# Three feed-forward first projections with both parts of the features in one 512-column matmul, and the two parts held in one tile

## The chip, the cores and the metric

The kernel runs on one core of one Trainium2 chip. The metric is the device time of one execution in microseconds (us). The engines named below are TensorE (PE for its matmuls, PEld for its weight loads), VectorE (DVE), ScalarE (ACT), GpSimd (POOL) and SyncE (SP, which issues most transfers). Matmuls write to PSUM, the accumulator memory; all other tiles lie in SBUF.

## What is computed

Two blocks run one after the other on 256 tokens with 1024 features. The first block has two layers; the second is one layer that also takes a context of 256 tokens and a condition vector.

```
# first block, for i in range(2):
h = h + concat(pool_mixer, dilated_attention)(rmsnorm(h, norm1[i]) @ w_in[i]) @ w_out[i]
hn = rmsnorm(h, norm2[i])
h = h + jnp.square(jax.nn.relu(hn @ w_up[i])) @ w_down[i]          # 1024 -> 4096 -> 1024
h = h + jax.nn.sigmoid(rmsnorm(h, norm3[i]) @ w_gate[i]) * (p[i] @ w_ple[i])
x = rmsnorm(h, final_norm)
# second block
mod = silu(c) @ w_mod + b_mod                                      # six shifts, scales and gates
h = modulate(x, norm1_g, sh1, sc1); hc = modulate(ctx, ...)
x = x + g1 * branch_merge(h, bidirectional gated delta scan(hc, h), short conv, fourier) @ w_o
a, b = split(modulate(x, norm2_g, sh2, sc2) @ w_ffn_in)            # 1024 -> 2 x 2816
x = x + g2 * ((silu(a) * b) @ w_ffn_out)
out = rmsnorm(x, final_g)
```

## The kernel before

Features lie on the 128 partitions (eight groups, `KD = 8`), the 256 tokens (`T`) along the free dimension. Every large product is made from fp32 values split in two parts, a high part and the rest: weights become `wh` and `wl` (in `weights`: ACT copies, DVE subtracts, in halves of 512 columns), features become `xh` and `xl` (in `split`). `mm3` then makes three matmuls of 256 moving columns for each 128x128 block: `wh` by `xh`, `wh` by `xl`, `wl` by `xh`. One unit of weights is 128x1024, which is eight such steps, 24 matmuls.

The work is a Python program that a scheduler turns into one order of instructions for each engine; each engine then runs its own in that order, and waits on semaphores for what others make. So an instruction that waits holds up all that stand behind it on its engine.

The stages, in order, with the stretch of the profiled execution in us: layer 0's attention with its out projection (0 to 117), its feed-forward `ffn` (to 304) and its gate (to 340); layer 1's the same (attention to 440, `ffn` to 657, gate to 692); the mixer of the second block (692 to 1010); its feed-forward `swiglu` (to 1203); the end. In `ffn`, 16 rounds each take two units of `w_up` into one PSUM bank (`cols_into`), make the squared relu in `square` (`fft`, `ah`, `al`), and take two units of `w_down` of the round before into four accumulators `acc` (`down`). In `swiglu`, 11 rounds each take four units of `w_fin`, and two of `w_fout`.

Three generators run beside these stages, one step at a time when `tick` is called for a unit: `modulation` (48 loads of `w_mod`, 512 KB each, through the tiles `wmst`; DVE multiplies each by a vector and sums), `context` and the delta recurrence (`dn_prep`, `dn_scan`). Inside `dn_prep`, `dn_base` inverts small blocks on POOL, with a way out to DRAM and back (`there`, `back`, `xc`), and then lets `trip` steps pass before `dn_merge` reads `xc` into `Tm` and `U` and multiplies with them:

```
        for _ in range(self.trip):
            yield
        X["X"] = xc
```

The normalization is not applied to the features but to the products: `row_steps` sums the squares of `h` (`ssp`, `ss`), takes the column sums on TensorE, makes the inverse root by DVE in ten small instructions (`rsv`, `rsy`, `rst`), and spreads it over the partitions (`across`); in `ffn` the first `square` needs that row. `residual` adds the accumulators to `h`, after which `norm_split` makes `xh` and `xl` of the next stage. `np2` sends the low part of the first three weights of the mixer (`wl`) to POOL in place of DVE.

## Time and profile before

| | |
|---|---|
| time, median of 3 runs | 1226.24 us (1225.2 to 1228.88) |
| the profiled execution | 1224.34 us, span 1222.2 us, mean granted TensorE clock 0.986 |
| PE busy | 1174.3 us (96%), 9882 matmuls |
| DVE busy | 899.3 us (74%) |
| ACT busy | 635.6 us (52%) |
| POOL busy | 119.9 us (10%) |
| moved by DMA | 221.43 MB |

Busy time of an engine is the time in which the profile shows an instruction on it; matmuls overlap, so the time that one matmul takes from the engine is read from how far apart the starts of neighbours lie, not from its own duration.

### The profile page before, as it was taken

Reading aid. Unit: us, or ns where it says so; the run is one execution under the profiler, and the core shown is the slowest. Engines: PE = TensorE matmul, PEld = TensorE weight load, DVE = VectorE, ACT = ScalarE, POOL = GpSimd, SP = SyncE. Lnnn points to the kernel's source line nnn. Section 1 sums busy time; section 2 is a strip of 40 time slices with the busy share of each in tenths; the row PEclk is TensorE's granted clock in tenths of the full one; section 3 lists DMA queues with packets and bytes.
Section 4 is the critical chain, followed back from the end, with each engine's and each line's share of the span. In section 5 each row is a group of like instructions: output and inputs, shape, how many; then the busy total and the mean of one; then the engine's idle time right before and its main releaser. Section 6 shows DMA issues by size and latency. Waiting matters only on the chain.

```text
span 1222.2 us, 24807 instructions
## 1 busy us (share of the span) xinstructions
PE 1174.3 (96%) x9882; PEld 1111.4 (91%) x9882; DVE 899.3 (74%) x1804; ACT 635.6 (52%) x1250; POOL 119.9 (10%) x207
## 2 busy tenths in 40 slices
PE   8999899999999989999999999997999999999997
PEld 6779899999977889999999979897989998999996
DVE  6998997556998488675657899897655768555555
ACT  5654645545755565644445555544333546544444
POOL 1000000000010000064000130275000000000000
PEclk9999999999999999999999989999999998999998
DMA  6767688555553645556444525677422452655552
GB/s 223 238 199 249 208 297 278 189 194 190 164 174 121 200 139 164 182 165 207 156 147 164 171 91 164 226 270 243 142 89 100 173 195 99 213 185 189 186 180 84
DMA packets 65779, 221.43 MB, mean 181 GB/s; under 512 B 10048, under 2 KB 11456, under 8 KB 65664
## 3 DMA queue, kind: packets, MB, share of 16 engines
q1 hardware_dynamic: 64800, 218.29, 53.4%
q0 software_dynamic: 864, 1.57, 0.6%
q8 instruction: 77, 1.26, 0.4%
q14 instruction: 38, 0.31, 0.1%
HBM read 218.00 MB, written 1.84 MB: 180 GB/s over the span
## 4 chain that ended last, share of the span: by engine, by line
PE 72%; DVE 13%; DMA 6%; POOL 4%; issue 3%; ACT 2%; SPq 0%; DVEq 0%; POOLq 0%; ACTq 0%
PE acc L274 38%; PE bank L274 33%; DVE wl L263 4%; DMA wmst<-w_mod 2%; DVE xl L298 1%; POOL bo L1288 1%; POOL bz L1289 1%; ACT wh L262 1%; DVE wmst L882 1%; PE bank L565 1%; DVE h L704 1%; DVE cy L1044 1%; DMA back<-bzt 1%; DVE qkT L533 1%; DMA pt<-pT 0%
## 5 line engine op out<-in xcount | busy, mean ns | idle before, releaser
L262 ACT ACTIVATE wh<-wst 128x512 fp32r<-128x512 f32 x708 | 411.9, 624 | 427.4 <-PE bank L274 157.3
L263 DVE TENSOR_TENSOR wl<-wst,wh 128x512 fp32r<-128x512 f32 x702 | 470.1, 703 | 208.5 <-ACT wh L262 208.0
L274 PE MATMUL bank<-xl,wh 128*128 128x256 f32 x992 | 280.5, 283 | 2.1 <-DVE xl L298 2.1
L274 PE MATMUL bank<-xh,wl 128*128 128x256 f32 x992 | 279.4, 282 | 2.9 <-DVE wl L263 2.9
L274 PE MATMUL bank<-xh,wh 128*128 128x256 f32 x992 | 281.3, 284 | 0.8 <-ACT wh L262 0.8
L274 PE MATMUL acc<-al,wh 128*128 128x256 f32 x688 | 191.6, 279 | 0.0
L274 PE MATMUL acc<-ah,wl 128*128 128x256 f32 x688 | 191.3, 279 | 0.0
L274 PE MATMUL acc<-ah,wh 128*128 128x256 f32 x688 | 191.2, 279 | 0.0
L274 PEld LDWEIGHTS bank<-xh,wl 128*128 128x128 f32 x992 | 187.0, 189 | 4.3 <-DVE wl L263 4.3
L274 PEld LDWEIGHTS bank<-xl,wh 128*128 128x128 f32 x992 | 187.0, 189 | 2.8 <-DVE xl L298 2.7
L274 PEld LDWEIGHTS bank<-xh,wh 128*128 128x128 f32 x992 | 187.1, 189 | 1.6 <-ACT wh L262 1.2
L274 PE MATMUL acc<-xh,wh 128*128 128x256 f32 x640 | 183.4, 287 | 2.2 <-ACT xh L911 2.2
L274 PE MATMUL acc<-xl,wh 128*128 128x256 f32 x640 | 182.0, 285 | 1.5 <-DVE xl L912 1.5
L274 PE MATMUL acc<-xh,wl 128*128 128x256 f32 x640 | 181.1, 284 | 0.5 <-DVE wl L263 0.4
L274 PEld LDWEIGHTS acc<-al,wh 128*128 128x128 f32 x688 | 129.0, 188 | 0.0
L274 PEld LDWEIGHTS acc<-ah,wl 128*128 128x128 f32 x688 | 128.9, 188 | 0.1
L274 PEld LDWEIGHTS acc<-ah,wh 128*128 128x128 f32 x688 | 128.9, 188 | 0.0
L274 PEld LDWEIGHTS acc<-xh,wh 128*128 128x128 f32 x640 | 121.6, 190 | 4.7 <-ACT xh L911 2.8
L274 PEld LDWEIGHTS acc<-xl,wh 128*128 128x128 f32 x640 | 121.5, 190 | 2.9 <-DVE xl L912 1.7
L274 PEld LDWEIGHTS acc<-xh,wl 128*128 128x128 f32 x640 | 121.9, 191 | 1.5 <-DVE wl L263 0.9
L274 PE MATMUL acc<-wl,xh 128*128 128x512 f32 x176 | 70.6, 401 | 2.5 <-DVE wl L263 2.4
L274 PE MATMUL acc<-wh,xh 128*128 128x512 f32 x176 | 70.8, 406 | 1.1 <-ACT wh L262 1.1
(365 smaller groups left out, 1564.8 us busy)
## 6 DMA issues: line engine op xcount, KB each, us to landing
wst<-w_up SPq DMA_DIRECT2D x64, 512.0 KB, 4.2
wst<-w_down SPq DMA_DIRECT2D x64, 512.0 KB, 4.2
wmst<-w_mod SPq DMA_DIRECT2D x48, 512.0 KB, 4.8
wst<-w_fin SPq DMA_DIRECT2D x44, 512.0 KB, 3.2
wst<-w_in SPq DMA_DIRECT2D x39, 512.0 KB, 3.6
wst<-w_mgate SPq DMA_DIRECT2D x24, 512.0 KB, 3.3
wst<-w_fout SPq DMA_DIRECT2D x22, 512.0 KB, 3.2
wst<-w_qkv SPq DMA_DIRECT2D x20, 512.0 KB, 3.4
```

The source lines that it names most:

```text
L262: nc.scalar.activation(wh[:, c:c + n], st[:, c:c + n], AF.Copy)
L263: i = (nc.gpsimd if self.onpool > 0 else nc.vector).tensor_tensor(wl[:, c:c + n], st[:, c:c + n], wh[:, c:c + n].bitcast(F32), op=OP.subtract)
L274: self.nc.tensor.matmul(out, lhsT, rhs, start=start, stop=stop, skip_group_check=skip)
L298: nc.vector.scalar_tensor_tensor(xl[:, k], src, gain, xh[:, k].bitcast(F32), op0=OP.mult, op1=OP.subtract)
L533: nc.vector.tensor_copy(qk[:, :, t * P:(t + 1) * P], bk.rearrange("p (c q) -> p c q", c=4))
L565: nc.tensor.transpose(bk[:, c * P:(c + 1) * P], s[:, g, c * P:(c + 1) * P], self.ident)
L704: self.nc.vector.tensor_add(h[:, js], h[:, js], acc[j][:, n[0]:n[1]])
L882: nc.vector.scalar_tensor_tensor(pr, st, 1.0, cv[v], op0=OP.mult, op1=OP.mult, accum_out=mod[:, part, v, k:k + 1])
L1044: nc.vector.scalar_tensor_tensor(y4[:, j], pad[:, j, :, tap:tap + CHUNK], w[:, j, tap:tap + 1], y4[:, j], op0=OP.mult, op1=OP.add)
L1288: pool.tensor_tensor(o, lt[:, c:, j:c].to_broadcast([P, n, c]), Z[:, j:c, 0:c].to_broadcast([P, n, c]), op=OP.mult)
L1289: pool.tensor_tensor(Z[:, c:, 0:c], Z[:, c:, 0:c], o, op=OP.subtract)
```

## The change

First, the two parts of the features are one tile (`Pair`, name `xs`), so that one access reaches both. Then the units of `w_up` and of `w_fin` (but for the first four of the latter) go through `wide` in place of `cols_into`: each step is one matmul with `wh` held and 512 moving columns (`xh` and `xl` side by side, into the two halves of a PSUM bank) and one with `wl` held and 256 columns. In all, 832 steps have two matmuls where they had three. A unit so takes a bank of its own, and `merged` adds the two halves: ACT copies one half to SBUF (104 times), DVE adds the other. In `ffn` the relu moves to ACT, and the row of the normalization is applied after `w_down`, in `residual`: the square of the inverse root is a plain reciprocal, so `mean_square_steps` takes the place of the root, in rounds 1, 3 and 5; `residual` gets a multiplication for each of its five pieces. The first round of `ffn` steps through two units side by side.

Beside that: `rotate` makes three larger DVE instructions where it made twelve; `g0` takes tiles of another pool; `np2` is 0, so that no weights are split on POOL; `trip` is 13; the 24 loads of parts 3, 4 and 5 of `modulation` leave the mixer, 8 of them for layer 0's and 16 for layer 1's `ffn`; the rate of `modulation` in layer 0 falls from 0.85 to 0.55 steps a unit; `context` lets four units pass before its column sums.

```diff
--- before.py
+++ after.py
+class Pair(list):
+    def __init__(self, both):
+        super().__init__((both[:, 0], both[:, 1]))
+        self.both = both
+class Quarters:
+    def __init__(self, make):
+        self.make, self.parts = make, {}
+    def __getitem__(self, key):
+        j = key[1].start // 2
+        if j not in self.parts:
+            self.parts[j] = self.make()
+        return self.parts[j]
...
     def pair(self):
-        return [self.act.tile([P, KD, T], F32R, name=n, tag="xs", bufs=4) for n in ("xh", "xl")]
+        return Pair(self.act.tile([P, 2, KD, T], F32R, name="xs", tag="xs", bufs=2))
...
     def rotary(self):
+        full = [self.b1.tile([P, 16, 2, 8], F32, name=n, bufs=1) for n in ("fcos", "fsin")]
+        for i in range(2):
+            for x in range(2):
+                for o, src, f in zip(full, (self.cos, self.sin), (1.0, 2.0 * x - 1.0)):
+                    nc.vector.tensor_scalar(o[:, 8 * i:8 * i + 8, x], src[:, i][:, None, :].to_broadcast([P, 8, 8]), f, None,
+                                            op0=OP.mult)
+        self.cos, self.sin = full
...
     def rotate(self, z):
-        w = [self.b1.tile([P, 2, 8, 8], F32, name=f"rot{j}", bufs=1) for j in range(4)]
-        for o, x, c in zip(w, (x1, x2, x2, x1), (co, si, co, si)):
-            for t in range(2):
-                nc.vector.tensor_mul(o[:, t], x[:, t], c[:, t])
-        for t in range(2):
-            nc.vector.tensor_sub(x1[:, t], w[0][:, t], w[1][:, t])
-            nc.vector.tensor_add(x2[:, t], w[2][:, t], w[3][:, t])
+        co, si = (self.b1.tile([P, 16, 2, 8], F32, name=f"rot{j}", bufs=1) for j in range(2))
+        nc.vector.tensor_mul(co, zz, self.cos)
+        nc.vector.tensor_mul(si, zz[:, :, ::-1], self.sin)
+        nc.vector.tensor_add(zz, co, si)
...
+    def wide(self, units, x, outer=False):
+        out = []
+        for us in (units,) if outer else [(u,) for u in units]:
+            w = []
+            for u in us:
+                self.tick()
+                w.append(self.weights(u))
+            bk = [self.bank2() for _ in us]
+            for k in range(KD):
+                for (h, l), b in zip(w, bk):
+                    ws = slice(k * P, k * P + P)
+                    for part in (1, 0) if k == KD - 1 else (0, 1):
+                        if part:
+                            self.mm(b[:, 0], l[:, ws], x[0][:, k], False, False, True)
+                        else:
+                            self.mm(b, h[:, ws], x.both[:, :, k], k == 0, k == KD - 1, True)
+            out += bk
+        return out
+
+    def merged(self, o, b):
+        c = self.sm.tile([P, T], F32, name="mt")
+        self.nc.scalar.activation(c, b[:, 1], AF.Copy)
+        self.nc.vector.tensor_add(o, b[:, 0], c)
...
-    def residual(self, acc):
+    def residual(self, acc, row=None):
         h = self.h
         for j in range(4):
             for n in ((0, 1), (1, 2)) if j == 3 else ((0, 2),):
                 js = slice(2 * j + n[0], 2 * j + n[1])
-                self.nc.vector.tensor_add(h[:, js], h[:, js], acc[j][:, n[0]:n[1]])
+                a = acc[j][:, n[0]:n[1]]
+                if row is not None:
+                    t = self.t2k("fft")[:, n[0]:n[1]]
+                    self.nc.vector.tensor_mul(t, a, row[:, None, :].to_broadcast([P, n[1] - n[0], T]))
+                    a = t
+                self.nc.vector.tensor_add(h[:, js], h[:, js], a)
+
+    def mean_square_steps(self, h, res):
+        nc = self.nc
+        ss = self.sumsq(h)
+        yield
+        v = self.sm.tile([P, 2], F32, name="rsv2")
+        nc.vector.tensor_scalar(v, self.col_sums((ss,)), 1.0 / D, EPS, op0=OP.mult, op1=OP.add)
+        nc.vector.reciprocal(v, v)
+        yield
+        r = self.sm.tile([P, T], F32, name="nrow")
+        nc.scalar.activation(r, self.across(v)[:, 0:T], AF.Copy)
+        res.append(r)
...
     def ffn(self, i):
-        def square(bv):
-            t = self.sm.tile([P, 2, T], F32, name="fft", tag="w2k", bufs=self.nw2k)
-            for n in range(2):
-                nc.vector.scalar_tensor_tensor(t[:, n], bv[:, n], 0.0, r[0], op0=OP.max, op1=OP.mult)
...
+        r = []
+        steps = self.mean_square_steps(self.h, r)
+        for f in range(16):
+            bv = self.wide([self.a["w_up"][i, 2 * f + n] for n in range(2)], x, f == 0)
+            if f in (1, 3, 5):
+                next(steps, None)
...
+            for n in range(2):
+                self.merged(t[:, n], bv[n])
+            nc.scalar.activation(t, t, AF.Relu)
             nc.scalar.activation(ah, t, AF.Square)
             nc.scalar.activation(t, t, AF.Square)
             nc.vector.tensor_sub(al, t, ah.bitcast(F32))
             pend.append((ah, al))
...
+            if f:
+                down(False)
+        self.residual(down(True), r[0])
...
-            self.beside(self.modulation(*self.mod_parts[0]), 0.85)
+            self.beside(self.modulation(*self.mod_parts[0]), 0.55)
...
     def context(self, d, e):
-        yield from self.modulate(Halves(hc), self.gains[:, 1], self.mod[:, 0, 1], x)
+        norm = self.modulate(Halves(hc), self.gains[:, 1], self.mod[:, 0, 1], x)
+        next(norm)
+        for _ in range(4):
+            yield
+        yield from norm
...
     def branches(self, x, hold):
-        g0 = self.act.tile([P, KD, T], F32, name="g0", tag="xs", bufs=4)
+        g0 = Quarters(lambda: self.t2k("g0"))
...
     def swiglu(self):
-                ab = []
-                for base in (0, NFF):
-                    bv = self.bank2()
-                    self.cols_into(bv, [self.a["w_fin"][base + 2 * f + n] for n in range(2)], x)
-                    ab.append(bv)
-                s = self.t2k("sw")
-                nc.scalar.activation(s, ab[0], AF.Silu)
-                nc.vector.tensor_mul(s, s, ab[1])
+                s, b = self.t2k("sw"), self.t2k("sb")
+                for base, o in ((0, s), (NFF, b)):
+                    for n in range(2):
+                        self.merged(o[:, n], self.wide([self.a["w_fin"][base + 2 * f + n]], x)[0])
+                    if base == 0:
+                        nc.scalar.activation(s, s, AF.Silu)
+                nc.vector.tensor_mul(s, s, b)
...
     def run(self):
-        self.np1 = 3
-        self.np2 = 3
+        self.np1 = 0
+        self.np2 = 0
...
-        self.trip = 10
-        self.mod_parts = (((1, 0, 2), (3,), (4, 5)), ((1, 0, 2), (), (3, 4, 5)), ((1, 0, 2, 3), (), (4, 5)), ((1, 0), (), (2, 3, 4, 5)))[1]
+        self.trip = 13
+        self.mod_parts = ((1, 0, 2, 3), (4, 5), ())
```

Three places show how this moves instructions. First PE, at the start of layer 0's `ffn`: the last matmuls of the out projection (`acc`) and the first of `w_up` (`bank`), before:

```order
L274 MATMUL acc<-xl,wh 128x256
L274 MATMUL acc<-xh,wl 128x256
L274 MATMUL bank<-xh,wh 128x256
L274 MATMUL bank<-xl,wh 128x256
L274 MATMUL bank<-xh,wl 128x256
```

and now, where two units alternate:

```order
L293 MATMUL acc<-xs,wh 128x256 x2
L293 MATMUL acc<-xs,wl 128x256
L293 MATMUL bank<-xs,wh 128x512
L293 MATMUL bank<-xs,wl 128x256
L293 MATMUL bank<-xs,wh 128x512
```

Three matmuls of 256 columns have become one of 512 and one of 256. Second DVE, at the same place: the adds of `residual` after the out projection, the splits of the eight feature groups (`xl` before, `xs` now), and what stands among them, before:

```order
L882 SCALAR_TENSOR_TENSOR wmst,mod<-wmst,cv_1274 128x1024
L263 TENSOR_TENSOR wl<-wst,wh 128x512 x2
L704 TENSOR_TENSOR h<-h,acc 128x512
L882 SCALAR_TENSOR_TENSOR wmpr,mod<-wmst,cv_1273 128x1024
L704 TENSOR_TENSOR h<-h,acc 128x512
L298 SCALAR_TENSOR_TENSOR xl<-h,k_norm_240,xh 128x256
L704 TENSOR_TENSOR h<-h,acc 128x512
L298 SCALAR_TENSOR_TENSOR xl<-h,k_norm_240,xh 128x256 x2
L704 TENSOR_TENSOR h<-h,acc 128x256 x2
L298 SCALAR_TENSOR_TENSOR xl<-h,k_norm_240,xh 128x256 x5
L317 TENSOR_TENSOR ssp<-sq 128x512
L263 TENSOR_TENSOR wl<-wst,wh 128x512
```

and now:

```order
L932 SCALAR_TENSOR_TENSOR wmst,mod<-wmst,cv_1249 128x1024
L758 TENSOR_TENSOR h<-h,acc 128x512
L282 TENSOR_TENSOR wl<-wst,wh 128x512
L758 TENSOR_TENSOR h<-h,acc 128x512
L318 SCALAR_TENSOR_TENSOR xs<-h,k_norm_248,xs 128x256 x2
L758 TENSOR_TENSOR h<-h,acc 128x512
L318 SCALAR_TENSOR_TENSOR xs<-h,k_norm_248,xs 128x256 x2
L758 TENSOR_TENSOR h<-h,acc 128x256 x2
L318 SCALAR_TENSOR_TENSOR xs<-h,k_norm_248,xs 128x256 x4
L282 TENSOR_TENSOR wl<-wst,wh 128x512 x5
```

The step of `modulation` between the first two adds is gone, the sums of squares stand further behind, and the weights of the second unit (the `wl` of the last row, from its second on) come after all splits. Third DVE, at the start of layer 0's gate, where the accumulators of `w_down` reach `h`, before:

```order
L704 TENSOR_TENSOR h<-h,acc 128x512 x2
L298 SCALAR_TENSOR_TENSOR xl<-h,k_norm_242,xh 128x256 x2
L704 TENSOR_TENSOR h<-h,acc 128x512
L298 SCALAR_TENSOR_TENSOR xl<-h,k_norm_242,xh 128x256 x2
L704 TENSOR_TENSOR h<-h,acc 128x256 x2
L298 SCALAR_TENSOR_TENSOR xl<-h,k_norm_242,xh 128x256 x4
```

and now:

```order
L756 TENSOR_TENSOR fft<-acc,nrow 128x512
L758 TENSOR_TENSOR h<-h,fft 128x512
L756 TENSOR_TENSOR fft<-acc,nrow 128x512
L318 SCALAR_TENSOR_TENSOR xs<-h,k_norm_250,xs 128x256
L758 TENSOR_TENSOR h<-h,fft 128x512
L756 TENSOR_TENSOR fft<-acc,nrow 128x512
L318 SCALAR_TENSOR_TENSOR xs<-h,k_norm_250,xs 128x256
L758 TENSOR_TENSOR h<-h,fft 128x512
L756 TENSOR_TENSOR fft<-acc,nrow 128x256 x2
L758 TENSOR_TENSOR h<-h,fft 128x256 x2
L318 SCALAR_TENSOR_TENSOR xs<-h,k_norm_250,xs 128x256 x6
```

Five multiplications have come in, and six of the eight splits, not four, stand behind the last add. Of layer 1's gate the order is the same, but there four DVE instructions of the context's `dn_merge` (`U`, `W`) now stand among its sums of squares. In the mixer, the order of PE between the last matmul of the latent `decay` (`gm` with `d_Cf`) and the first with `U` held 384 matmuls of 256 columns before, and holds 480 now.

## Rows read from the trace of the kernel before

**Rows 1.** The page, first part: busy us (share) and instructions.
```profile
PE 1174.3 (96%) x9882; PEld 1111.4 (91%) x9882; DVE 899.3 (74%) x1804; ACT 635.6 (52%) x1250; POOL 119.9 (10%) x207
```
**Rows 2.** Stretches: us, busy PE, PEld, DVE, ACT, POOL, clock, DMA share, GB/s.
```profile
117.00:145.00 28.00, 23.62 (x186) 22.20 (x185) 26.95 (x60) 16.56 (x32) 0.00 (x0) 1.00 0.60 216
145.00:190.00 45.00, 45.00 (x386) 45.00 (x385) 40.16 (x74) 22.47 (x40) 0.00 (x0) 1.00 0.86 292
...
440.00:456.00 16.00, 11.98 (x83) 11.04 (x83) 15.04 (x44) 10.17 (x22) 0.00 (x0) 0.89 0.39 132
456.00:657.00 201.00, 200.34 (x1939) 197.79 (x1938) 133.42 (x259) 104.07 (x201) 38.73 (x80) 1.00 0.53 170
...
692.00:760.00 68.00, 61.84 (x543) 55.33 (x542) 65.89 (x154) 36.65 (x94) 19.04 (x40) 0.95 0.36 120
760.00:847.00 87.00, 82.34 (x701) 79.26 (x700) 81.31 (x149) 43.22 (x96) 45.49 (x65) 0.98 0.78 263
```
**Rows 3.** Chain of waits, pieces with only matmuls: start us, us, count.
```profile
224.13 5.65 PE bank L274 x48
229.78 5.44 PE acc L274 x48
...
363.96 5.77 PE acc L274 x25
...
564.61 5.72 PE bank L274 x48
...
1051.57 11.44 PE bank L274 x96
```
**Rows 4.** Waits of PE, 106 to 146 us: total us, times, longest.
```profile
PE bank L274 <- DVE xl L298: 2.1, 3, 1.3
PE bank L370 <- DVE rsy L361: 1.2, 1, 1.2
```
**Rows 5.** Timeline of DVE, start of layer 0's `ffn`: start us, us, instruction, idle before.
```profile
119.50 1.22 DVE L882 SCALAR_TENSOR_TENSOR wmpr<-wmst,cv 128x1024 f32<-128x1024 f32 x1 [0.86 <-DMA wmst<-w_mod]
```
**Rows 6.** Waits of PE, 438 to 458 us: total us, times, longest.
```profile
PE bank L274 <- DVE rsy L358: 3.4, 1, 3.4
```
**Rows 7.** Timeline of DVE, start of layer 0's gate: start us, us, instruction, idle before.
```profile
305.94 0.68 DVE L704 TENSOR_TENSOR h<-h,acc 128x512 f32<-128x512 f32 x1
306.54 0.88 DVE L298 SCALAR_TENSOR_TENSOR xl<-h,k_norm,xh 128x256 fp32r<-128x256 f32 x2
307.33 0.74 DVE L704 TENSOR_TENSOR h<-h,acc 128x256 f32<-128x256 f32 x2
307.99 1.72 DVE L298 SCALAR_TENSOR_TENSOR xl<-h,k_norm,xh 128x256 fp32r<-128x256 f32 x4
309.62 0.69 DVE L317 TENSOR_TENSOR ssp<-sq 128x512 f32<-128x512 f32 x1
```
**Rows 8.** Waits of PE, 690 to 860 us: total us, times, longest.
```profile
PE bank L274 <- DVE U L1317: 5.4, 1, 5.4
PE acc L274 <- ACT xh L911: 2.2, 2, 1.3
```
**Rows 9.** Chain of waits, start of the mixer: start us, us.
```profile
694.70 1.26 POOL wl L263
```
**Rows 10.** Instructions on `wmst` alone, two stretches: busy DVE, ACT; clock; DMA share.
```profile
692.00:760.00 68.00, 5.68 (x9) 0.00 (x0) 0.95 0.36 120
760.00:847.00 87.00, 23.59 (x38) 0.00 (x0) 0.98 0.78 263
```
**Rows 11.** Groups of instructions by line, shapes apart: busy us, mean ns, idle before.
```profile
L262 ACT ACTIVATE wh<-wst 128x512 fp32r<-128x512 f32 x708 | 411.9, 624 | 427.4 <-PE bank L274 157.3 <-PE acc L274 139.8 <-issue 51.0
L716 DVE SCALAR_TENSOR_TENSOR fft<-bank,nrow 128x256 f32<-128x256 f32 x64 | 24.4, 419 | 21.7 <-PE bank L274 21.4 <-ACT nrow L404 0.2
L1105 ACT ACTIVATE tokv<-bank 128x256 f32<-128x256 f32 x8 | 3.0, 378 | 6.0 <-PE bank L1104 5.9
L519 DVE TENSOR_TENSOR rot<-zqk,rcos 128x64 f32<-128x64 f32 x24 | 5.3, 221 | 0.9 <-ACT zqk L507 0.8
```

More of the change, by code (lines that the diff above doesn't have):

```diff
@@ L373, in norm_split @@
     def norm_split(self, h, gain):
-        xh, xl = self.pair()
+        x = self.pair()
         for k in range(KD):
-            self.split(h[:, k], k, gain(k), xh, xl)
-        return xh, xl
+            self.split(h[:, k], k, gain(k), *x)
+        return x
     def norm_cols(self, h):
@@ L511, in rotate @@
         nc = self.nc
-        zz = z.rearrange("p t (h d) -> p t h d", d=HD)
-        x1, x2 = zz[:, :, :, 0:8], zz[:, :, :, 8:16]
-        co = self.cos[:, :, None, :].to_broadcast([P, 2, 8, 8])
-        si = self.sin[:, :, None, :].to_broadcast([P, 2, 8, 8])
-        w = [self.b1.tile([P, 2, 8, 8], F32, name=f"rot{j}", bufs=1) for j in range(4)]
-        for o, x, c in zip(w, (x1, x2, x2, x1), (co, si, co, si)):
-            for t in range(2):
-                nc.vector.tensor_mul(o[:, t], x[:, t], c[:, t])
-        for t in range(2):
-            nc.vector.tensor_sub(x1[:, t], w[0][:, t], w[1][:, t])
-            nc.vector.tensor_add(x2[:, t], w[2][:, t], w[3][:, t])
+        zz = z.rearrange("p t (h d) -> p (t h) d", d=HD)[:, :, 0:16].rearrange("p n (x j) -> p n x j", x=2)
+        co, si = (self.b1.tile([P, 16, 2, 8], F32, name=f"rot{j}", bufs=1) for j in range(2))
+        nc.vector.tensor_mul(co, zz, self.cos)
+        nc.vector.tensor_mul(si, zz[:, :, ::-1], self.sin)
+        nc.vector.tensor_add(zz, co, si)
     def scores(self, i, b, z, S):
@@ L722, in square @@
             pend.append((ah, al))
-        r = []
-        steps = self.row_steps_sb(self.h, r)
-        next(steps)
-        wait = []
-        for f in range(16):
-            bv = self.bank2()
-            if f == 0 and self.ko & 4:
-                self.cols_into(bv, [self.a["w_up"][i, n] for n in range(2)], x, True)
-            for n in range(2):
-                if f or not self.ko & 4:
-                    self.cols_into(bv[:, n:n + 1], [self.a["w_up"][i, 2 * f + n]], x)
-                if f == self.at[0] and n == self.at[1]:
-                    next(steps)
-                if f == self.at[2] and n == self.at[3]:
-                    run(steps)
-                    for b in wait:
-                        square(b)
-                    wait = None
-            if wait is not None:
-                wait.append(bv)
-            else:
-                square(bv)
-                while len(pend) > 1:
-                    down(False)
-        self.residual(down(True))
+            if f:
+                down(False)
+        self.residual(down(True), r[0])
     def ple(self, i):
@@ L1412, in dn_scan, with half_pair @@
         res.append(S)
-    def half_pair(self, name):
-        t = self.act.tile([P, KD, T], F32R, name=name, tag="xs", bufs=4)
+    def half_pair(self, n):
+        t = self.halves2[:, n]
         return t[:, 0:4], t[:, 4:8]
@@ L1518, in dn_output @@
         nc = self.nc
-        y = self.half_pair("ydn")
+        y = self.half_pair(1)
         ot = [o.rearrange("p h c -> p (h c)") for o in ot]
@@ L1612, in branches @@
         yield from self.zgate(x, z)
-        ysc = self.half_pair("ysc")
+        self.halves2 = self.act.tile([P, 2, KD, T], F32R, name="ys", tag="xs", bufs=2)
+        ysc = self.half_pair(0)
         yield from self.short_conv(x, ysc)
@@ L1622, in branches @@
             yield
-        yfn = self.half_pair("yfn")
+        yfn = self.half_pair(1)
         yield from self.fourier(x, yfn)
@@ L1661, in ahead @@
         nc = self.nc
-        U = [self.act.tile([P, KD, T + 2], F32R, name=n, tag="xs", bufs=4) for n in ("uh", "ul")]
+        U = Pair(self.act.tile([P, 2, KD, T + 2], F32R, name="us", tag="xs", bufs=2))
         sh = self.sm.tile([P, KD, 2], F32, name="ush", bufs=1)
@@ L1720, in swiglu @@
             else:
-                ab = []
-                for base in (0, NFF):
-                    bv = self.bank2()
-                    self.cols_into(bv, [self.a["w_fin"][base + 2 * f + n] for n in range(2)], x)
-                    ab.append(bv)
-                s = self.t2k("sw")
-                nc.scalar.activation(s, ab[0], AF.Silu)
-                nc.vector.tensor_mul(s, s, ab[1])
+                s, b = self.t2k("sw"), self.t2k("sb")
[5 more added lines that the diff above has]
+                nc.vector.tensor_mul(s, s, b)
             ah = self.sm.tile([P, 2, T], F32R, name="ah", tag="w2k", bufs=self.nw2k)
```

## The prediction

> **What bounds the kernel now.** I read the page first: PE is busy for 96% of the span, DVE for 74%, ACT for 52% [rows 1]. A busy PE isn't yet one that could be no faster, so the second view is the table of stretches. It shows two kinds. In the middle of the feed-forward stages PE has no gap (45.0 of 45 us, 200.3 of 201), while DVE works two thirds of the time and ACT half in the longer one. At the starts of stages and in the mixer PE has gaps and DVE is nearly full: 26.95 of 28 us, 15.04 of 16, 65.89 of 68, 81.31 of 87 [rows 2]. So there are two ways to save time: PE's own pace in the full stretches, and what DVE has ahead of PE's next operand in the others. The third view, the chain of waits, gives the pace: 48 matmuls of 256 columns take 5.65 us in layer 0's first projection (117.7 ns each), 5.72 in layer 1's and the same in the last feed-forward (11.44 for 96, 119.2 ns each), and 25 of 512 columns take 5.77 us (230.8 ns each) [rows 3]. The clock is granted in full there, the level of 2.4 GHz [rows 2]. The fourth view, the waits of PE, names what ends each gap.
>
> **The wide matmul.** It applies to 832 steps: 256 in each layer's feed-forward, 320 in the last. Each had three matmuls of 256 columns and gets one of 512 and one of 256. The trace has 512-column matmuls only with features held and weights moving; I take their pace, since the size is the same. A step of layer 0 goes from 3 x 117.7 to 230.8 + 117.7 ns, 4.6 ns less; one of the other two from 3 x 119.2 to 230.8 + 119.2, 7.6 ns less. Sum: 256 x 4.6 + 576 x 7.6 = **5.6 us less**. Bounds: nothing, if 512 columns cost two of 256 exactly; and 13.5 us, if the step keeps the pace of the fastest piece, 5.44 us for 48 [rows 3], which is 340 ns a step (13 ns less in 256 steps, 17.5 in 576). The columns to be moved stay 768 a step, so leaving out a third of the weight loads (busy 91% [rows 1], but beside the matmuls) can't give more than that pace.
>
> [...]
>
> **Getting out of PSUM.** New on ACT: 104 copies of 128x256 out of PSUM, 0.38 us each by the nearest row, and 32 relus of 512 columns, which cost what other 512-column activations do (0.62): 59 us. On DVE 104 adds of 256 columns stand where 64 like operations and ten larger ones stood (0.42 each [rows 11]), some 10 us more. I cost both at nothing: ACT is busy 104 of 201 us in layer 1's feed-forward, DVE 133 [rows 2], and a bank is needed again only three or four units later. Without that cover each unit would pay its 0.38 + 0.42 us, 83 us in all; this is the rival on the other side, below.
>
> **The starts of the two feed-forwards.** From 117 to 145 us 186 matmuls ran, which at 117.7 ns is 21.9 us: 6.1 us lost. From 440 to 456 us 83 ran, 9.9 us: 6.1 lost [rows 2, 3]. At the first PE waits 2.1 us for the splits, most of it because a `modulation` step that itself waited 0.86 us for its load stands among the adds, and 1.2 us for the root [rows 4, 5]; at the second 3.4 us for a column sum that came behind a root [rows 6]. The change takes all three away: that step is no longer there, the root is, in `ffn`, a reciprocal needed only at the end, and the context's sums come later. What is late next is the low part of the second unit's weights, since two units now alternate. On DVE stand from the first add on: three adds and one pair of halves (3 x 0.60 + 0.66), eight splits (3.2) [rows 7], and three halves of `wl` at 0.60 in layer 0 (one of them among the adds), one in layer 1: 7.4 and 6.2 us. PE has 36 matmuls of the out projection and three of the first step to do meanwhile, 4.8 us. So 2.6 and 1.4 us stay lost, and for the context's sums I leave 0.5 in layer 1. Gain: 3.5 + 4.2 = **7.7 us less**. Bounds: nothing (DVE just as late) and all 12.2.
>
> **The ends of the two feed-forwards.** `residual` now multiplies before it adds: 3 x 0.60 + 0.66 = 2.5 us more of DVE per layer. Before, one pair took an add and two splits, 0.60 + 0.79 us, about what PE needs for a pair of accumulators (12 matmuls, 1.4 us), and the last split ended at 309.62 [rows 3, 7]. There is no slack, so I take the whole: **4.9 us more**. Bounds: nothing, and 8 us, if the four `U` and `W` instructions of 0.6 us that now stand among the sums of layer 1's gate are paid too.
>
> **The mixer.** PE waits 5.4 us for `U` [rows 8], whose blocks come back from DRAM late; DVE waits in order for the same transfer. With `trip` at 13 PE has 96 more matmuls ahead of it, 11.3 us at 118 ns, so the wait goes: **5.4 us less**; bounds 3 and 5.4. The scan still ends before the last gate units, by the order of PE. Besides, PE idles 6.2 us between 692 and 760 and 4.7 between 760 and 847 [rows 2]. There 29.3 us of `modulation` on DVE go away [rows 10], and three splits on POOL, 1.26 us each on the chain [rows 9], become 3.6 us on a full DVE. I take **4 us less**; bounds 4 more and 10.9 less. The moved loads (24 of 512 KB) now issue from SP among those of `w_up` and `w_down`: 16 in layer 1's 201 us make 42 GB/s on top of 170, while PE had no gap at 292 GB/s [rows 2]; so nothing for that.
>
> **Rotations.** 72 small DVE instructions of 0.22 us become 18 larger of 0.42 [rows 11], 8 us of DVE less, but PE waited there mostly for others, and eight small ones come in at the very start: **1 us less**, bounds 1 more and 4 less.
>
> **Sum.** -5.6 - 7.7 + 4.9 - 5.4 - 4 - 1 = -18.8. From the profiled execution's 1224.34 that is 1205.5; its time lies 1.9 us under the median of the runs, 1226.24, so against that **1207 us**.
>
> **The rivals.** (1) Columns are cheaper in the mixed pattern: the wide steps keep the fast pace (13.5, not 5.6), and half of the mixer's remaining 7 us goes too: 1207 - 8 - 4 = 1195. For it: the same shapes ran at 113 ns in one stage [rows 3]; against: only there. Chance 0.15. (2) The starts move rather than shrink: the alternating units wait as long as before (0 for 7.7), layer 1's gate pays the merge (8), the mixer's DVE stays as late (0 for 4) and 512 columns cost two of 256 (0 for 5.6). That leaves -5.4 - 1 + 8, 1228, the same within the 0.3% (3.7 us) that a measurement of this kernel can tell. For it: DVE is full at each of these places. Chance 0.10. (3) Slower: the copies stand in ACT's queue, where each waits for its unit's last matmul and the `wh` halves of a later unit stand behind it. If a unit's weights get late by one half, 0.62 us [rows 11], 104 units lose 65 us: 1272. It decides from 18.8 / 104 = 0.18 us a unit. Against it: three units' weights are kept, so such a half waits for the same matmul anyway, and before, DVE's `fft` waited 21.4 us for its banks [rows 11] in stretches where PE had no gap. Chance 0.06.
>
> Beside the third: the Trainium skill ("ScalarE: Activation LUTs", section "Rules for kernel authors") puts relu and add on VectorE, not ScalarE, and so speaks against moving the relu. The rows have 0.62 us for 512 columns on ACT against 2 x 0.42 on DVE, and ACT is the emptier one.
>
> **How the numbers follow.** The forecast, 1207, has 0.57, with 1200 to 1214 as its own range. The rest, 0.12, is a smaller gain (1214 to 1222: the starts or the mixer give half). The range reaches from the first rival to the edge of no change, 1194 to 1222, which leaves out the second and third and the tail of the first. Faster by over 0.3%: 0.84; within: 0.10; slower: 0.06.
>
> **What would show it.** Right: 32 matmuls (two units) of a projection in 5.6 us, which is 350 ns a step; no wait of PE for `rsy` in either feed-forward, and none for `U` in the mixer; waits of 1 to 3 us at both feed-forward starts for `wl` and at both gate starts for `xs`. Wrong: PE idle in the middle of a feed-forward, with `wh` behind an ACT copy `mt`; a step at 355 ns or more; waits of PE in the mixer as long as now.

## The result, and the profile after

The changed kernel takes **1212.02 us** (median of 4 runs, 1211.11 to 1214.47), beside 1225.72 of the kernel before on the same chip: a ratio of 0.9888, 95% interval 0.9865 to 0.9911, 13.7 us less. The forecast was 1207 with a range of 1194 to 1222: the direction and the range hold, and the gain is 5 us smaller than its sum. The profiled execution (1214.47 us, span 1212.7) is the slowest of the four; the spans of the other three are 1209.3 to 1210.5. What the traces show as lost or gained in one stage has a scatter of its own, and the experiments give its size.

The page, first part; it answers to [rows 1]. A twelfth of the matmuls is gone, and PE is busy for as long as before:

```profile
PE 1173.5 (97%) x9050; PEld 1073.9 (89%) x9050; DVE 913.1 (75%) x1800; ACT 685.6 (57%) x1386; POOL 103.5 (9%) x201
```

The stretches, columns as in [rows 2], cut where the stages now lie. PE's gap of 4 us in the third is gone, the last two have less idle PE, and the last has much less DVE (63.5 us in place of 81.3):

```profile
117.00:145.00 28.00, 26.85 (x176) 23.88 (x175) 27.36 (x52) 20.38 (x42) 0.00 (x0) 1.00 0.65 218
145.00:190.00 45.00, 45.00 (x323) 42.11 (x322) 39.80 (x74) 27.58 (x53) 0.00 (x0) 1.00 0.90 313
440.00:456.00 16.00, 16.00 (x111) 14.78 (x111) 13.69 (x27) 13.41 (x27) 0.00 (x0) 1.00 0.51 157
456.00:648.00 192.00, 188.26 (x1518) 175.46 (x1518) 147.63 (x294) 115.47 (x236) 42.59 (x80) 0.99 0.66 211
690.00:760.00 70.00, 65.31 (x597) 59.31 (x596) 64.40 (x174) 44.30 (x119) 9.10 (x36) 1.00 0.33 106
760.00:847.00 87.00, 85.72 (x736) 83.06 (x735) 63.54 (x112) 42.93 (x82) 37.23 (x66) 1.00 0.58 173
```

The chain of waits, pieces with only matmuls, as in [rows 3]; `bank` x32 is two units (16 steps), x64 four:

```profile
231.27 5.58 PE bank L293 x32
236.85 5.66 PE acc L293 x48
242.50 5.56 PE bank L293 x32
...
1061.08 11.20 PE bank L293 x64
1072.29 5.65 PE acc L293 x48
```

A step takes 349 ns in layer 0 (5.58 / 16) and 350 in the last feed-forward (11.20 / 32), as forecast. Layer 1's pieces aren't on the chain; the starts of its matmuls lie 232.5 and 116.8 ns apart, 349 a step.

PE's waits in three stretches: 106 to 146 us and 298 to 312 us (the starts of layer 0's feed-forward and gate), and 690 to 1000 us (the mixer). They answer to [rows 4] and [rows 8]; `rsy` and `U` are gone, and `dr` is new. At the start of layer 0's feed-forward PE waits for `wh`, not for `wl` as forecast:

```profile
PE bank L293 <- ACT wh L281: 1.1, 2, 0.6
...
PE bank L293 <- DVE xs L318: 1.7, 1, 1.7
...
PE bank L293 <- DVE dr L1429: 4.5, 2, 2.3
PE acc L293 <- ACT xs L961: 1.5, 2, 1.1
```

Between 436 and 456 us the same view shows no wait at all [rows 6].

To see where the time went I cut both traces, and those of the experiments, at the last matmul into the accumulators of each stage. In us, from the profiled execution of each kernel; layer 1's feed-forward, its gate and the mixer are one column, since the context's recurrence runs across that edge:

| | attention 0 | `ffn` 0 | gate 0, attention 1 | `ffn` 1, gate 1, mixer | `swiglu` | end |
|---|---|---|---|---|---|---|
| before | 120.1 | 186.9 | 131.5 | 574.7 | 197.6 | 11.4 |
| after | 118.9 | 185.1 | 134.1 | 567.8 | 195.5 | 11.4 |
| difference | -1.2 | -1.8 | +2.6 | -6.9 | -2.1 | 0 |
| the forecast's terms there | -0.5 | -4.7 | +2.0 | -13.1 | -2.4 | 0 |

Two columns miss, `ffn` 0 and the long one. In the first, DVE now waits for loads of `w_mod` in the middle of the stage (chain of waits; the low parts of two units stand behind them, and PE waits 0.8 us twice):

```profile
198.20 6.83 DMA wmst<-w_mod
205.13 0.13 DVE wmst L932
205.26 1.02 issue
206.37 0.34 DVE fft L723
206.70 0.91 DVE wl L282 x2
```

In layer 1's feed-forward the moved `modulation` stands among the steps of the context's convolution (the wait of PE for `kT`, then the timeline of DVE):

```profile
PE bank L1167 <- DVE kT L1138: 2.5, 1, 2.5
...
508.00 0.69 DVE L282 TENSOR_TENSOR wl<-wst,wh 128x512 fp32r<-128x512 f32 x1
508.77 1.67 DVE L1098 SCALAR_TENSOR_TENSOR cy<-pad,k_dn_conv,cy 128x256 f32<-128x256 f32 x4
510.37 0.68 DVE L282 TENSOR_TENSOR wl<-wst,wh 128x512 fp32r<-128x512 f32 x1
510.97 1.21 DVE L932 SCALAR_TENSOR_TENSOR wmst<-wmst,cv 128x1024 f32<-128x1024 f32 x1
512.11 0.08 DVE L932 DVE_READ_ACCUMULATOR wmst<-wmst,cv 128x1 f32 x1
512.11 0.75 DVE L1138 SCALAR_TENSOR_TENSOR kT<-cth,cy 128x256 f32<-128x256 f32 x2
```

And in the mixer the scan waits. The chain at the first of the two `dr` waits:

```profile
877.89 5.84 PE acc L293 x47
883.73 0.02 issue
883.75 0.64 ACT wh L281
884.39 0.02 issue
884.42 0.69 DVE wl L282
885.11 0.60 DVE dr L1428
885.71 0.65 DVE wl L282
886.36 0.61 DVE dr L1429
```

DVE has `dr` ready to make, but in its queue the low half of a later unit stands ahead of each of the two instructions; that half waits for ACT's high half, ACT waits for a buffer, and PE frees the buffer with its last matmul ahead of the one that needs `dr`. So nothing overlaps, and PE stands still for 2.2 us; 20 us later the same happens again, 2.3 us.

The waits are not the whole price. Behind each of them the clock granted to TensorE is down at its lower level, 1.2 GHz, for most of the next 7 us. The same 58 matmuls, from the first with `dr` to the last of that scan step, take 7.34 us at a granted clock of 0.54 here, and 4.57 us at 1.00 in `e1_three_256` (below), where PE had waited 2.2 us for `dr` too (windows view, columns as in [rows 2]):

```profile
887.02:894.36 7.34, 7.34 (x59) 5.79 (x59) 1.38 (x2) 0.60 (x1) 0.00 (x0) 0.54 0.24 71
...
898.49:903.06 4.57, 4.35 (x58) 3.48 (x58) 1.29 (x2) 0.60 (x1) 0.00 (x0) 1.00 0.37 115
```

The second place is the same (7.42 us at 0.54), so in this execution the two waits cost some 10 us, of which 4.5 are the waits. As `e1` shows, the clock does not fall behind every such wait.

### The profile page after: what moved, and what is told of

It is laid out like the page before. It is cut to its first block, busy times and chain, and to the rows that moved or that the text cites. A ratio compares the mean times of both kernels' runs of the same rounds, so it can differ in the third digit from the quotient of the medians.

```text
span 1212.7 us, 23326 instructions
## 1 busy us (share of the span) xinstructions
PE 1173.5 (97%) x9050; PEld 1073.9 (89%) x9050; DVE 913.1 (75%) x1800; ACT 685.6 (57%) x1386; POOL 103.5 (9%) x201
## 4 chain that ended last, share of the span: by engine, by line
PE 65%; DVE 13%; issue 11%; DMA 4%; POOL 3%; ACT 2%; SPq 0%; DVEq 0%; POOLq 0%; ACTq 0%
PE acc L293 39%; PE bank L293 25%; DVE wl L282 4%; DMA wmst<-w_mod 2%; DVE cy L1098 1%; DVE wmst L932 1%; DMA wst<-w_down 1%; ACT wh L281 1%; PE bank L587 1%; POOL bo L1342 1%; POOL bz L1343 1%; DVE xs L318 0%; DVE S L566 0%; DVE qkT L555 0%; PE bank L390 0%
## 5 line engine op out<-in xcount | busy, mean ns | idle before, releaser
L293 PE MATMUL bank<-xs,wh 128*128 128x512 f32 (+1 forms) x1152 | 353.6, 367 | 3.2 <-DVE xs L318 1.7
L293 PE MATMUL bank<-xs,wl 128*128 128x256 f32 x992 | 262.7, 282 | 2.1 <-DVE wl L282 2.1
L293 PE MATMUL acc<-xs,wh 128*128 128x256 f32 x1280 | 236.8, 285 | 1.7 <-ACT xs L961 1.1
L293 PEld LDWEIGHTS bank<-xs,wh 128*128 128x128 f32 x1152 | 203.7, 190 | 32.2 <-ACT wh L281 2.8
L293 PEld LDWEIGHTS acc<-xs,wh 128*128 128x128 f32 x1280 | 199.3, 191 | 5.0 <-issue 1.4
L293 PEld LDWEIGHTS bank<-xs,wl 128*128 128x128 f32 x992 | 188.1, 190 | 11.3 <-DVE wl L282 4.2
L293 PE MATMUL acc<-xs,wl 128*128 128x256 f32 x640 | 181.1, 283 | 0.0
L293 PEld LDWEIGHTS acc<-xs,wl 128*128 128x128 f32 x640 | 122.0, 191 | 0.5 <-issue 0.2
L293 PE MATMUL acc<-wh,xs 128*128 128x512 f32 x352 | 116.0, 402 | 0.9 <-ACT wh L281 0.9
L293 PE MATMUL acc<-wl,xs 128*128 128x512 f32 x176 | 70.2, 399 | 2.8 <-DVE wl L282 2.8
L932 DVE SCALAR_TENSOR_TENSOR wmst<-wmst,cv 128x1024 f32<-128x1024 f32 x48 | 59.1, 1232 | 13.1 <-DMA wmst<-w_mod 12.7
```

What stands on the lines that cost most here:

```text
L293: self.nc.tensor.matmul(out, lhsT, rhs, start=start, stop=stop, skip_group_check=skip)
L932: nc.vector.scalar_tensor_tensor(pr, st, 1.0, cv[v], op0=OP.mult, op1=OP.mult, accum_out=mod[:, part, v, k:k + 1])
```

## The experiments

Twelve kernels. Theory one is the prediction's: each term is what its step says, and `trip` takes the `U` wait away. The rival, formed on the trace after: the moved `modulation` takes the `U` wait away, and `trip` only makes the scan late.

**The width.** `e1_three_256`:

```diff
-                            self.mm(b, h[:, ws], x.both[:, :, k], k == 0, k == KD - 1, True)
+                            self.mm(b[:, 0], h[:, ws], x[0][:, k], k == 0, k == KD - 1, True)
+                            self.mm(b[:, 1], h[:, ws], x[1][:, k], k == 0, k == KD - 1, True)
```

> The changed kernel with each 512-column matmul of the three projections replaced by two of 256 columns (high part, low part) into the two halves of the same bank; banks, copies, adds and all else stay. Theory of the prediction: the width itself gives 4.6 to 7.6 ns a step, so this is 5.6 us slower than the changed kernel, about 1217.6, and two units take 5.65 to 5.72 us again in place of 5.56 to 5.60. Rival 1: the pace hangs on how the rest lies (two other kinds of matmul changed their pace without an edit), and the width gives nothing: within 2 us of 1212. Rival 2: the width gives the fast pace somewhere the trace hides: 10 us slower or more.

The sums of this kernel aren't those of the changed one, so only its times are read; matmuls and data moved are as expected. Measured: 1224.12 us (ratio 0.9976, 0.996 to 0.9993), 12 us over the changed kernel. The chain of waits, the pieces that answer to those above:

```profile
234.97 5.76 PE bank L293 x48
240.74 5.66 PE acc L293 x48
...
1068.09 11.53 PE bank L293 x96
```

Per two units 0.19 us more in layer 0's 16 rounds, per four 0.33 in 10 rounds of the last feed-forward, and 10 ns a step in layer 1 (359 beside 349, by the starts of the matmuls; 256 steps): 3.0 + 3.3 + 2.6 = 8.9 us, 11 ns a step. Neither the first theory's 5.6 nor rival 1: the width counts, and three matmuls that alternate between the halves of a bank (120 ns each) are slower here than the three into one region that stood there before (117.7 and 119.2 [rows 3]); that the alternation is the reason is not shown. Against the pieces of the kernel before the width is worth (5.65 - 5.57) x 16 + (5.72 - 5.59) x 16 + (11.44 - 11.20) x 10 = 5.8 us, beside the forecast 5.6. Rival 2's number, 10 us or more, came out by the medians, but not its reason: the pace of these pieces lies open in the trace. The spans of the two profiled executions differ by 9.5 us (1222.2 and 1212.7), so pace is nearly all of it; the 12 by the medians hold the 2.45 us by which the changed kernel's profiled execution lies over its median.

**Rotations.** `e4_rotate_before` puts the body of `rotate` and its small tables back (the minus and plus lines of the change's diff exchanged).

> The changed kernel with the twelve small instructions of the rotation of the kernel before. Theory of the prediction: 1 us slower (1213), in the two attention stages. Rival 1: DVE is what PE waits for there and its 8 us less count half: 4 us slower (1216). Rival 2: the new tables at the start cost what the rotations save: within 1 us of 1212 or faster.

Measured: 1214.95 us, ratio 0.99 (0.9878 to 0.9921), beside 0.9888: 1.5 us slower, which lies within the intervals, so the total alone tells the forecast's 1 us neither from nothing nor from rival 1's 4. By stages attention 0 is 1.0 longer and the column with attention 1 0.4, which speaks for the forecast. `ffn` 0 is 3.0 longer, for another reason: in this kernel's order of DVE a step of `modulation` again stands between the first two adds of `residual`, as in the kernel before, and again waits for its load (timeline of DVE):

```profile
120.30 1.23 DVE L930 SCALAR_TENSOR_TENSOR wmpr<-wmst,cv 128x1024 f32<-128x1024 f32 x1 [1.96 <-DMA wmst<-w_mod]
```

PE then waits 2.7 us for `xs`, as it does not in the changed kernel. So this run, without meaning to, also takes back a part of the starts, and where that step stands hangs on edits elsewhere.

**The ends.** `e7_no_row`:

```diff
-        self.residual(down(True), r[0])
+        self.residual(down(True))
```

> The changed kernel without the multiplication by the row in residual of both feed-forwards; the features so lack that normalization from there on, all else stays. Theory of the prediction: the multiplication is paid in full at both ends, 2.5 us each, so this is 4.9 us faster (about 1207), and the wait of 1.9 us for xs at layer 0's gate is gone or under 0.5. Rival: DVE is late there for another reason (the splits and halves beside it), and this gives under 1.5 us.

Measured: 1210.67 us (ratio 0.9873, 0.9852 to 0.9894), 1.4 us under the changed kernel by the medians. From the last matmul into the accumulators to DVE's first instruction on a gate's products it is 12.6 and 13.2 us before, 15.4 and 16.1 after, and 13.5 and 14.4 here. So the two ends cost 5.7 us (forecast: 4.9), and the multiplications make 3.6 of it. The wait for `xs` at layer 0's gate is gone, as expected. In the total less arrives: a sum between both theories.

**`trip` and `modulation`, two by two.** The edits are the two lines below (and the rate, 0.55 to 0.85), in the changed kernel, alone and together:

```diff
-        self.trip = 13
-        self.mod_parts = ((1, 0, 2, 3), (4, 5), ())
+        self.trip = 10
+        self.mod_parts = ((1, 0, 2), (), (3, 4, 5))
```

> The changed kernel with trip at 10. Theory of the prediction: the 5.4 us wait for U comes back in the mixer and nothing else changes there: about 1217.4. Rival, from the trace after: at 13 the scan's steps come later and PE waits 2.4 and 2.5 us for dr, with some 3.5 us of small gaps around them, so at 10 these go as the U wait comes back: 5.4 - 8.4 = -3, about 1209. Either way PE waits for U over 3 us in the mixer; the two theories differ in whether the dr waits near 885 and 905 us are gone.

> The changed kernel with the modulation parts and rate of the kernel before: parts 3, 4 and 5 run in the mixer again, none in layer 1's feed-forward, and layer 0's run at 0.85 steps a unit. Theory of the prediction: the moved loads cost nothing in the feed-forwards and give most of the mixer's 4 us, so this is 3 to 5 us slower, 1215 to 1217. Rival, from the trace after: in the feed-forwards DVE now comes late (PE waits of 1.0 and 1.0 us for wl near 206 and 218, of 2.7, 0.8 and 0.6 us near 510 to 529), some 6 us, so this is faster in the feed-forwards by 4 to 6 and slower in the mixer by 4 to 8: 1210 to 1216, with these feed-forward waits gone.

> The changed kernel with both the modulation (parts and rate) and trip of the kernel before; with the changed kernel, trip at 10 alone and the modulation of before alone it makes a table of two by two. Theory that the modulation sets when U is back: the inversion on POOL takes over 20 us again and the U wait is back at 3 to 6 us, the dr waits are gone: 1212 to 1216, so 4 to 8 slower than with trip at 10 alone. Rival (trip alone decides): the U wait would have been back with trip at 10 alone, where PE had none, so this rival has only chance left; it expects the same time as with trip at 10 alone, within 3 us of 1208.

| | `trip` 10 | `trip` 13 |
|---|---|---|
| parts 3 to 5 in the mixer | 1214.5 us; `U` 5.8, no `dr` (`e8`) | 1212.24; `dr` 4.4 in two waits (`e3`) |
| parts 3 to 5 in the feed-forwards | **1208.15**; neither (`e2`) | 1212.02; `dr` 4.5 in two waits (the change) |

With `trip` at 10 alone PE has no wait for `U` and none for `dr`; all four runs (1207.33 to 1209.96) lie under all four of the changed kernel, ratio 0.9852 (0.9833 to 0.987). With `e9` below it is the fastest kernel here that leaves nothing out. My expectation that the `U` wait would be there was wrong under both theories. In the long column of the stage table it has 562.9 us beside 567.8. The table also shows that each edit alone takes the `U` wait away: `trip` in `e3` (0.5 us of it are left, though the inversion still takes 22.7 us there), the moved parts in `e2`. Only `trip` puts `dr` in its place. And with `trip` at 13 the moved parts are worth nothing in the total (1212.24 and 1212.02; the six runs of `e3` scatter from 1207.51 to 1217.22).

The same two edits on the kernel before, each alone (`trip` 10 to 13; the parts and the rate):

> The kernel before with only trip changed, from 10 to 13. Theory of the prediction: 96 more matmuls stand ahead of U, its 5.4 us wait goes and nothing takes its place: about 1221. Rival, from the trace after: the wait goes, but the recurrence comes three steps later, so the scan's dr is late where PE has less left beside it and 5 to 8 us come back: within 4 us of 1226, with waits for dr of over 2 us near 885 to 925 us.

> The kernel before with only the modulation parts and rate of the changed kernel (trip stays 10). Theory of the prediction: moving the loads relieves DVE at the mixer's start, at most 4 us, and PE still waits 3 us or more for U, since trip is what takes that wait away: 1222 to 1226. Rival, from the traces: with DVE less full the inversion on POOL takes 15 to 17 us in place of the 22 to 24 us between blt and bzt, so xc is back some 20 us earlier and the U wait goes with trip at 10; the mixer is 8 to 12 us shorter, layer 1's feed-forward 4 to 6 us longer and layer 0's up to 3: 1219 to 1224.

Measured: 1227.11 us with `trip` alone (ratio 1.0005, 0.9984 to 1.0026): nothing. Waits of PE, 690 to 1000 us:

```profile
PE bank L274 <- DVE dr L1375: 4.9, 3, 2.3
...
PE bank L274 <- DVE U L1317: 0.9, 2, 0.7
```

What `U` gives, `dr` takes. With `modulation` alone 1223.04 us (0.9962, 0.9948 to 0.9976): neither wait is over 0.2 us, the long column is 6.0 us shorter (568.7), and `ffn` 0 is 3.3 longer (190.2), which is also the size of that stage's scatter. From `blt` to `bzt` it is 15.8 us, as the rival has it, but `xc` lands only 5 us earlier than in the kernel before (847.0 beside 851.7; 10 us counted from the end of layer 1's feed-forward), not 20.

**What makes `U` late.** `e12_loads_only` is `e8` with the 24 loads left where they are, but without DVE's work on them:

```diff
+                        if part > 2:
+                            nc.vector.tensor_copy(mod[:, part, v, k:k + 1], st[:, 0:1])
+                        else:
                             nc.vector.scalar_tensor_tensor(pr, st, 1.0, cv[v], op0=OP.mult, op1=OP.mult,
```

> The kernel of the two by two table with modulation and trip of before (U wait of 5.9 us, inversion on POOL 23 us from blt to bzt), but for parts 3, 4 and 5 DVE's multiplication of 128x1024 (1.2 us, 24 of them in the mixer) is replaced by a copy of one column; the sums of these parts so are left out, and the 24 loads stay where they are. Theory that DVE's two-operand work slows POOL: with 24 to 29 us of it less the inversion takes 15 to 18 us, xc is back 5 us or more earlier, the U wait is under 1.5 us and the time 1206 to 1210. Rival: the traffic of the 24 loads delays the way over DRAM and the inversion: the inversion stays over 20 us, or xc still takes 8.5 us or more after bzt, the U wait stays over 4 us and the time at 1211 to 1214.

Measured: 1202.54 us (0.9803, 0.9783 to 0.9822), no wait for `U`, and faster than its theory's range: 12 us under `e8`. The stretch from `blt` to `bzt`, in which POOL makes the inversion, in the windows view, with the groups of POOL's products `bo` in it below. First `e8`:

```profile
806.62:829.35 22.73, 22.43 (x187) 22.23 (x186) 21.89 (x43) 11.26 (x21) 20.25 (x32) 1.00 0.89 302
...
L1342 POOL TENSOR_TENSOR bo<-blt,bz 128x15 f32<-128x15 f32 (+7 forms) x15 | 11.5, 765 | 1.2
```

then `e12`:

```profile
801.39:816.36 14.97, 14.97 (x127) 14.97 (x126) 9.73 (x20) 8.33 (x16) 12.48 (x32) 1.00 0.95 348
...
L1345 POOL TENSOR_TENSOR bo<-blt,bz 128x15 f32<-128x15 f32 (+7 forms) x15 | 5.6, 376 | 1.2
```

and `e2`, with neither loads nor their work:

```profile
804.48:819.43 14.95, 14.95 (x127) 14.95 (x126) 9.93 (x16) 8.07 (x16) 12.47 (x32) 1.00 0.60 184
```

The same 30 small instructions of POOL take 22.7 us beside a full DVE (21.89 busy) and 15.0 beside one that is busy for 9.7 or 9.9; that the transfers run at 348 or 184 GB/s changes nothing. So the traffic is not what lengthens the inversion, DVE's work is. The way back over DRAM, from the start of `bzt` to the landing of the last `xc`, takes 13.4 us in `e8`, 15.7 in `e12` and 13.6 in `e2`: it is no shorter without the work. `xc` lands 10.7 us earlier in `e12` than in `e8` (832.0 and 842.7); 7.8 of that is the inversion and 5.2 that it begins earlier, less 2.3 by the way back.

The traces also hold single pairs. First `e8`: a product of POOL begins inside one of DVE's multiplications and ends just after it; then the same product in `e12`, with nothing on DVE:

```profile
807.16 1.24 DVE L932 SCALAR_TENSOR_TENSOR wmst<-wmst,cv 128x1024 f32<-128x1024 f32 x1 [1.28 <-DMA wmst<-w_mod]
807.40 1.07 POOL L1342 TENSOR_TENSOR bo<-blt,bz 128x15 f32<-128x15 f32 x1
...
802.16 0.22 POOL L1345 TENSOR_TENSOR bo<-blt,bz 128x15 f32<-128x15 f32 x1
```

In the four kernels with this work in the mixer (before, `e3`, `e5`, `e8`), 24 of POOL's products and sums of the inversion begin inside such a multiplication; each takes 1.07 to 1.33 us and ends 0.07 to 0.17 us after it. Where no DVE instruction overlaps them, they take 0.22 to 0.32 us.

**Variations around the best.** Half of the moved loads back in the mixer (`mod_parts` `((1, 0, 2, 3), (4,), (5,))`), POOL's share back (`np2` 3), and `trip` at 8, the first two with `trip` at 10:

> The changed kernel with trip at 10 and the moved loads divided: part 4 (8 loads) stays in layer 1's feed-forward, part 5 (8 loads) goes back to the mixer. Theory that the modulation sets when U is back, by DVE's load during the inversion on POOL: these 8 come at the mixer's start and are done before the inversion, so it still takes 15 to 17 us from blt to bzt and PE has no wait for U; layer 1's feed-forward loses half of what the loads cost it (4.6 us by the two runs with and without them): 1204 to 1208, against 1208 with trip at 10 alone. Rival: any load in the mixer makes the inversion late, and the U wait is back with 2 us or more: 1209 to 1213.

> The changed kernel with trip at 10 and np2 at 3, so that POOL makes the low parts of the mixer's first three weights again. Theory of the prediction: these three as 3.6 us of a full DVE against 1.26 us each on the chain come out even: within 2 us of 1208. Rival 1: they were among what made the mixer's start slow (PE waits of 1.6 and 1.8 us for xh and xl in the kernel before, 1.3 and 0.5 in the changed one): 2 to 4 us slower. Rival 2: DVE is what PE waits for at the mixer's start, so POOL's help is worth 2 us.

> The changed kernel with trip at 8. At 10 xc is back 5.5 us before DVE reads it, and two steps are some 7 us, so by the theory that U's wait is xc's return against the place of the step PE waits 1 to 2 us for U, and no dr wait comes back: 1207 to 1211. Rival: later steps are only lost, as from 10 to 13 (4 us for three steps), and 8 gains 2 to 3 more: about 1205.

`e9`: 1208.52 us (0.9854, 0.9831 to 0.9877), the same as `e2`; POOL takes 15.0 us from `blt` to `bzt` and `U` has no wait, as the first theory has it. Layer 1's feed-forward is 4.4 us shorter than in `e2` and the mixer 3.3 longer; the rest of the gain is within what stages scatter. `e10`: 1214.54 us (0.9898, 0.9878 to 0.9918), 6.4 us slower than `e2` (5.6 by the two ratios): rival 1, and more than it said. PE's waits at the mixer's start are about as long as in the kernel before (2.2 us for `xh` [rows 8], and the first line here for `xl`; `e2` has 0.8 and 0.6). The two lines of `e10` stand below it:

```profile
PE acc L274 <- DVE xl L912: 1.5, 1, 1.5
...
PE acc L293 <- ACT xs L961: 1.9, 1, 1.9
PE acc L293 <- DVE xs L962: 1.5, 1, 1.5
```

Of the 5.4 us that PE loses there against `e2`, 3.8 lie in the gaps around these waits and 1.6 behind them, where the granted clock is 0.50 from 707.7 to 714.5 us. The same stretch at that place is in all four kernels with `np2` at 3 (before, `e5`, `e6`, `e10`), and in none with 0.

`e11`: 1215.88 us (0.9911, 0.9891 to 0.9931), slower than both theories said. DVE reads `xc` no earlier than with 10 (834.1 us, beside 833.1 in `e2`), though two steps fewer are passed, because it already stands waiting for the transfer (timeline of DVE):

```profile
834.14 0.76 DVE L1371 TENSOR_TENSOR Tm<-xc,k_d_blk 128x256 f32<-128x256 f32 x2 [2.84 <-DMA xc<-back]
```

In `e2` that wait of DVE is 0.82 us, so at 10 the read already comes when `xc` lands; the 5.5 us to spare in the expectation were counted from the end of the issue of these transfers, not from their landing. With 8 DVE only stands still earlier, and all behind it in its queue with it. One wait of 2.3 us for `dr` is back; what makes the rest of the 7.7 us is open.

## Why the prediction was right, and where its size was off

- **The wide matmul (-5.6)**: right, 5.8 by pace. One thing next to it was missed: from 230 us on, layer 0's second projection ran at 5.44 us for 48 before [rows 3], and at 5.66 after. Over its 768 matmuls the starts lie 117.8 ns apart in place of 115.3, 1.9 us given back. Why is open.
- **Getting out of PSUM (0)**: right. No row shows PE behind an ACT copy `mt`; the slower rival (1272) falls.
- **The starts (-7.7)**: the waits went as forecast or better (1.4 us are left in layer 0 by the gaps between matmuls, nothing in layer 1), though what is left is for `wh`, not `wl`. Of layer 1's 6.1 us before, some 2 were not a wait: the granted clock fell to 0.5 for 3.4 us at 450 us, behind the wait for `rsy`, which is the 0.89 in [rows 2]. No run takes the starts back by themselves; `e4` does so by chance for layer 0's. In layer 0 part of it was given back in the middle, below.
- **The ends (+4.9)**: right, 5.7.
- **Rotations (-1)**: 1.4 by the two attention columns; the total can't tell it from 0 or 4.
- **"The moved loads ... so nothing for that"**: the first wrong step. I looked at the transfers alone, and not at the DVE instruction of 1.2 us behind each, nor at what stands behind that. In the changed kernel, layer 1's feed-forward is 4.6 us longer with them (214.5 beside 209.9 in `e3`, which has no wait for `kT`). In layer 0 the loads themselves come late in some executions: six kernels with the same program up to there show 182.2 to 185.5 us for `ffn` 0.
- **The mixer, `U` (-5.4)**: the second wrong step, "with `trip` at 13 PE has 96 more matmuls ahead of it ... so the wait goes". The matmuls ahead were counted; that the scan moves by the same steps was dismissed ("the scan still ends before the last gate units"). Alone on the kernel before, `trip` gives 0 (0.9984 to 1.0026), and with the other edits it costs 3.9 us. The wait for `U` does go with it, but waits for `dr` come. The wait would have gone without it: with `modulation` gone from DVE, POOL begins the inversion earlier and takes 15.4 us from `blt` to `bzt` in place of 24.0; the last `xc` lands at 830.7 us, before at 851.7 (the stage ahead ends 7.7 us earlier, too). In the changed kernel it then lies there for 12.5 us, until DVE reads it at 843.2.
- **The rest of the mixer (-4)**: too small. `np2` alone is worth 6.4 us (`e10` to `e2`). `modulation` out of the mixer is worth 6.4 too with `trip` at 10 (`e8` to `e2`), but most of that is the term before: by the starts of the same matmuls the mixer gets 12 us shorter, 8 at the wait for `U` (5.8, and the slow clock behind it) and 4 ahead of it, and layer 1's feed-forward 5.5 longer. The prediction held POOL's three splits for even with DVE's, since it priced them by their durations; PE's two waits of 1.9 and 1.5 us in `e10` show that they were on the path. One wait in the view behind [rows 8] is in none of its rows: 2.8 us for `tokk`, of which 0.3 are left after.

So the sum came near by luck in part, because two errors have opposite signs: too little for the mixer's relief, too much for `trip` and the loads. The clock behind a wait of PE stands in none of its terms. With `trip` left at 10 the forecast's 1207 is met within 1.2 us.

The Trainium skill ("SBUF — State Buffer", section "SBUF: two separate sides") has a rule that bears on the inversion: VectorE and GpSimd share one pair of ports as an exclusive lock, and a VectorE instruction with two SBUF inputs and a GpSimd one that reads SBUF block each other for the whole instruction. The runs agree as far as they reach: POOL's mean is 765 ns beside a full DVE and 376 beside the emptier one. The instruction left out in `e12` has two inputs in SBUF, and in the 24 pairs above POOL ends only when DVE's instruction has; what POOL does to DVE was not measured.

## What to carry to other kernels

When work is moved off a full engine, look at whom that engine slows, not only at who waits for it: here the gain of moving DVE's work arrived through POOL. A delay that is put in to hide a wait is worth testing again after every other edit, since the wait may have gone by another way and the delay then only moves what follows. And a late step in one queue is priced by what stands ahead of it there: a prefetch that waits for a buffer cost the scan 2.2 and 2.3 us, and each time the clock cost nearly 3 more. Last, a transfer is back when it has landed, not when its issue ends: taking one for the other made `xc` look 5 us early.

## What the runs showed of the hardware

- POOL's small products (128x15 to 128x64, two operands) take 765 ns in the mean beside a DVE that is 96% busy and 370 to 376 beside one that is busy for 65 or 66%, whatever the DMA traffic (184 or 348 GB/s); the sums between them take 543 and 415 to 418. One that begins inside a 1.2 us multiplication of DVE with two inputs in SBUF ends 0.07 to 0.17 us after it (24 of 24).
- Three 256-column matmuls that alternate between the two halves of a PSUM bank start 120 ns apart; with both halves in one 512-column matmul the pair takes 232.5 ns, and the single one after it 117.
- Behind a wait of PE of 2.2 or 2.3 us the granted clock was 0.54 over the next 7.3 us in the changed kernel, and 58 matmuls took 2.8 us longer than behind the same wait in `e1`, where it stayed at 1.00.
- `ffn` 0 with the same program varies by 3.3 us among six kernels (DMA share 0.75 in the changed kernel, and 0.90 from 145 to 190 us), while gate 0 and attention 1 (share 0.52) repeat within 0.4 (134.0 to 134.4 us in nine kernels with the same program there). That the loads are the reason is not shown.
